# A mixture-of-experts stage in units of 32 slots instead of 64

## The chip, the cores and the metric

The kernel runs on one core of a Trainium2 chip. The metric is the device time of one execution in microseconds; the time before is 2393.91 us, the median of three runs (2392.5 to 2396.63). The profile shows one further execution. Engines are named PE (TensorE), DVE (VectorE), ACT (ScalarE), POOL (GpSimd) and SP (SyncE, which issues the DMAs of the weights).

## The reference

A float32 model of four mixer layers is followed by a second block: an adaptive norm, a hybrid mixer, and a layer of 32 experts of which each of the 256 tokens uses four. The change touches only the experts:

```
logits = xt @ w_router + b_router                  # 256 tokens x 32 experts
top_v, top_e = lax.top_k(logits, 4)
gates = softmax(top_v)
for each expert e, for its tokens:
    h = xt @ w1[e] + b1[e]                         # 1024 -> 2048
    gate, up = split(h);  gate = min(gate, 7);  up = clip(up, -7, 7)
    h = gate * sigmoid(1.702 * gate) * (up + 1)    # the swiglu, 1024 wide
    y[token] += gates[token, e] * (h @ w2[e] + b2[e])   # 1024 -> 1024
out = rms_norm(x + gate2 * y, final_norm)
```

How many tokens an expert gets is known only when the kernel runs. Each expert's w1 has 8 MB and its w2 4 MB.

## The kernel before

Everything up to the router (until about 1297 us) is the same in both kernels and is left out here. The expert stage walks over the experts in order (`for e in range(32)`, L1929 to L1964). The place of a token in an expert is a slot. The first 64 slots of an expert are always computed; slots 64 to 95, 96 to 127 and 128 upwards stand in branches that test the count `n` of the expert (`tc.If(n > 64)`, nested `n > 96` and `n > 128`), in `up_others` and `down_others`.

One expert goes through these steps:

- Gather: one-hot matrices P (token by slot, one column per slot) are multiplied with the tokens (`g<-P,xc`) for two experts at a time; the result, modulated, is `xq`, 64 slots of each.
- `up_proj`: slots (64 columns of the array) against w1. The bias of `b1` is the first product (`hg<-b1p,sel`). The 2048 columns of w1 are four blocks; with 64 slots two blocks lie on the two column halves of the array at once, and the result `hg` covers two banks, [128, 2, 512].
- swiglu on DVE and ACT into `um` [128, 512], four transposes of `um` into `aT` (`act_T`, L1739).
- `down_proj` of the expert before (`py<-w,aT`, L1748): two column halves; its output is scaled by the slots' gates (`slot_gates`, tile `gsq`) and by gate2, and split into two parts `yeh` and `yel`.
- `scatter`, once per pair of experts (even iterations): the transposed one-hots `gTq` times `yeh` and `yel` (`py<-yeh,gTq`) sum 128 slots over all rows of the array into the tokens' `y`, which lies in `xl`; DVE adds.
- A branch repeats the same in units of 32 slots, each block of w1 on a quarter of the columns (`hg<-w,xs`), with its own gather before it and its own sum behind it (`down_more`).

Weights come through a ring of 18 tiles of 1 MB: eight of w1 (`wload`, L1405) and four of w2 (L1411, L1418 for the last expert) for each expert, in the order w1[0], w1[1], w2[0], w1[2], w2[1] and so on, all issued by SP. A tile may be overwritten when its readers are done. For w1 that includes the branch: SP waits for the place where all engines are past the branch "up" of the expert (L1899, called its join here), for w2 for that of "down" (L1885). Into the same queue, ahead of the last four tiles of w1 of expert 31, goes the small load of the final norm's weights, `fr` (L1916), which waits for its own buffer.

The order of instructions on each engine is fixed when the kernel is built, by a scheduler with hints (`tc.issue_after`, `announce`). On each engine what stands behind a waiting instruction waits too.

Of the kernel before, what the change touches and what calls it, by code (L numbers as in the profile page):

```python
# [51 lines left out]
def tile_model(ctx: ExitStack, tc: tile.TileContext, A, out):  # L52
# [1368 lines left out]
    def w2_tile(e, kk, hh):  # L1421

        if e < 31:
            return w2s[e][kk // 2][:, kk % 2, hh * 512:(hh + 1) * 512]
        return w2s[e][2 * hh + kk // 4][:, kk % 4, :]
# [31 lines left out]
    def gate_halves():  # L1457

        g2 = rt["g2"] = rt["pool"].tile([128, 512], F32, name="g2")
        p = rtile(1, 512)  # L1460
        for b in range(2):
            mm(p[64 * b:64 * b + 64], selg[:, 2 * b:2 * b + 1].to_broadcast([128, 64]), mods[5][2])
        evac(g2, p)
# [97 lines left out]
    def new_P():  # L1561
        return rt["pool"].tile([128, 2, 128], F32, name="P2", tag="P2")
# [3 lines left out]

    def block(hg, b):
        if len(hg.shape) == 2:  # L1570
            return hg[32 * b:32 * b + 32, :], 32
        return hg[64 * (b % 2):64 * (b % 2) + 64, b // 2, :], 64

    def bias(e, hg):
        for b in range(4):
            o, n = block(hg, b)
            r = 4 * (e % 8) + b
            i = mm(o, rt["late"][1][:, r:r + 1].to_broadcast([96, n]), rt["late"][0][:, e // 8], True, False)
        return i
# [34 lines left out]
    def route():  # L1614
# [5 lines left out]
        with tc.issue_after(rt["last"].ins):  # L1620
            gather_first(0, 4)
            gate_halves()
# [14 lines left out]
    def experts(pos, gate, num):  # L1637
        h = xc
        with ExitStack() as st:
# [5 lines left out]
            def add_b2():  # L1645

                g2f = ep.tile([128, 1024], F32, name="g2f", tag="yeh")
                tmps = ep.tile([128, 1024], F32, name="tmps", tag="yel")
                for b in range(2):
                    p = gtile()  # L1650
                    mm(p, ident[:, 64 * b:64 * b + 1].to_broadcast([128, 128]), g2)
                    evac(g2f[:, b * 512:(b + 1) * 512], p)
                g4, gT = [tmps[:, 512 * i:512 * i + 512].rearrange("p (a b) -> p a b", b=128) for i in range(2)]
                V.memset(g4, 0.0)
                for t in range(2):
                    tp = gtile()
                    for c in range(4):
                        V.tensor_copy(g4[:, c, 32 * c:32 * c + 32], gate[:, t])
# [34 lines left out]
            def transposed(P, dst):  # L1693

                p = gtile()
                for t in range(2):
                    T.transpose(p[:, t * 128:(t + 1) * 128], P[:, t], ident)
                evac(dst, p[:, 0:256])

            def slot_gates(P, e, gs):  # L1700

                p = gtile()
                for j in range(2):
                    for t in range(2):
                        for hh in range(2):
                            mm(p[64 * hh:64 * hh + 64, j:1 + j], P[:, t, slices(j)], gate[:, t, e + j:e + j + 1], t == 0, t == 1)
                V.tensor_copy(gs, p[:, 0:2])
# [11 lines left out]
            def up_proj(w1, hg, xs, k0=0, k1=8):  # L1719
                for k in range(k0, k1):  # L1720
                    for b in range(4):
                        i = mm(block(hg, b)[0], xs[:, k, :], w1[k][:, b * 512:(b + 1) * 512], False, k == 7)
# [20 lines left out]
            def down_proj(aT, e, gs, take):  # L1743

                p = ytile()
                for kk in range(8):
                    for hh in range(2):
                        i = T.matmul(p[64 * hh:64 * hh + 64, :], aT[:, kk % 4, 64 * (kk // 4):64 * (kk // 4) + 64],  # L1748
                                     w2_tile(e, kk, hh), start=kk == 0, stop=kk == 7)
                        if kk == hh == 0:  # L1750
                            announce(i, f"down{e}")
                for hh in range(2):
                    sl = slice(hh * 512, (hh + 1) * 512)
                    rs = slice(64 * hh, 64 * hh + 64)
                    take(sl, p[rs, :], gs[rs], g2[rs])
                return i

            def scatter(gT, ye):

                for t in range(2):  # L1760
                    for hh in range(2):
                        sl = slice(hh * 512, (hh + 1) * 512)
# [26 lines left out]
            def act_more(hgs, g, um):  # L1789
                swiglu(hgs[g][0:64], hgs[g][64:128], um[half(g)], half(g))  # L1790

            def down_more(e, j, g, um, ps):
# [5 lines left out]
                p = ps[1]  # L1798
                for kk in range(8):
                    for hh in range(2):  # L1800
                        r = 64 * hh + 32 * (kk % 2)
                        i = mm(p[r:r + 32, :], aT1[:, kk % 4, 32 * (kk // 4):32 * (kk // 4) + 32],
                               w2_tile(e, kk, hh), kk < 2, kk > 5)
                        if kk == hh == 0:
                            first = i
                P1 = new_P1()
                for t in range(2):
                    at = ep.tile([128, 1], F32, name="ats", tag="ats")
                    V.tensor_scalar(at, pos[:, t, e:e + 1], -float(64 * j + 32 * g), None, ALU.add)
                    for i in range(2):  # L1810
# [415 lines left out]
```

## Time and profile before

| | before |
|---|---|
| time, median of 3 runs | 2393.91 us |
| profiled execution | 2408.4 us |
| its span | 2406.5 us |
| granted TensorE clock, mean | 0.96 |
| TensorE busy | 2226.5 us, 93% |
| VectorE busy | 1188.2 us, 49% |
| ScalarE busy | 725.9 us, 30% |
| up projection, `hg<-w,xq` | 500.2 us in 2048 instructions |
| down projection, `py<-w,aT` | 221.3 us in 992 instructions |

The matmuls of float32 stand twice in the trace for each one in the program, so 64 rows of the trace are 32 products. A matmul's time in a timeline is from its start to a modelled end, and several run at once in different parts of the array. Shares over the whole span say little here, as the stages differ; what counts is the expert stage from 1297 us on.

### The profile page before, as it was taken

To read this page: it belongs to the slowest core of one execution; us is meant where nothing else is said; L and a number is where in the kernel's file an instruction comes from. 1 tells how busy PE (TensorE), PEld (TensorE's weight loads), DVE (VectorE), ACT (ScalarE), POOL (GpSimd) and SP (SyncE) were. 2 spreads that over 40 slices of the span, in tenths; PEclk is the share of its full clock that TensorE was granted. 3 is DMA by queue.
4 is the path that set the end of the run, shared out by engine and by line. 5 is a ranking of instruction groups with operands and counts; after the bars stand their busy time and mean duration, and the time that the engine had idled before them with its cause. 6 is when DMAs were issued, how large, how long until landed. Compare 5 with 4: busy or idle time off the path is not lost. (4 is left out here: it accounts for less than half of the span.)

```text
span 2406.5 us, 32540 instructions
## 1 busy us (share of the span) xinstructions
PE 2226.5 (93%) x12516; PEld 1372.9 (57%) x12516; DVE 1188.2 (49%) x2545; ACT 725.9 (30%) x1588; POOL 79.8 (3%) x125
## 2 busy tenths in 40 slices
PE   7999999999999999998998899989989899999997
PEld 4767777777788887677864343333334333334342
DVE  3877666656666669867544123232323333322332
ACT  3555454345333456554232011010111110101101
POOL 0000010000000010002200000000000000000000
PEclk9999999999999999999999899999989989999998
DMA  8443432333333245646237978787999868999995
GB/s 305 132 149 127 136 119 78 98 125 125 115 102 122 80 127 180 206 162 249 80 111 305 371 312 351 281 350 278 413 414 415 333 257 354 378 413 413 413 377 230
DMA packets 124828, 576.71 MB, mean 240 GB/s; under 512 B 11953, under 2 KB 12721, under 8 KB 91762
## 3 DMA queue, kind: packets, MB, share of 16 engines
q1 hardware_dynamic: 124530, 572.71, 62.5%
q8 instruction: 190, 3.11, 0.5%
q14 instruction: 108, 0.88, 0.1%
HBM read 571.61 MB, written 1.05 MB: 238 GB/s over the span
## 5 line engine op out<-in xcount | busy, mean ns | idle before, releaser
L136 PE MATMUL hg<-w,xq 128*64 128x512 f32 x2048 | 500.2, 621 | 15.2 <-PEq L1899 6.7
L136 PE MATMUL mm<-hT,wp 128*128 128x256 f32 (+1 forms) x1776 | 351.2, 342 | 0.6 <-DVE aqk L144 0.5
L136 PEld LDWEIGHTS hg<-w,xq 128*64 128x64 f32 x2048 | 161.1, 143 | 323.3 <-issue 306.3
L136 PEld LDWEIGHTS mm<-hT,wp 128*128 128x128 f32 x1776 | 272.5, 190 | 54.2 <-issue 19.8
L1729 DVE TENSOR_SCALAR gm<-hg 128x512 f32<-128x512 f32 (+1 forms) x37 | 25.6, 691 | 436.2 <-PE hg L136 434.6
L1748 PE MATMUL py<-w,aT 128*64 128x512 f32 x992 | 221.3, 592 | 1.1 <-DMA w<-w 1.0
L111 DVE TENSOR_TENSOR wp<-w,wp 128x1024 fp32r<-128x1024 f32 (+2 forms) x149 | 178.7, 1204 | 75.5 <-ACT wp L110 72.1
L136 PE MATMUL mm<-wp,hT 128*128 128x256 f32 (+1 forms) x1584 | 198.1, 284 | 5.1 <-DVE mixT L419 3.0
L136 PEld LDWEIGHTS mm<-wp,hT 128*128 128x128 f32 x1584 | 191.0, 191 | 11.0 <-DVE mixT L419 3.2
L110 ACT ACTIVATE wp<-w 128x1024 fp32r<-128x1024 f32 (+2 forms) x149 | 153.8, 1035 | 101.3 <-PE mm L136 55.2
L1730 ACT ACTIVATE um<-gm 128x512 f32<-128x512 f32 x32 | 20.2, 630 | 528.8 <-DVE gm L1729 528.8
L1748 PEld LDWEIGHTS py<-w,aT 128*64 128x64 f32 x992 | 84.3, 137 | 131.0 <-issue 118.9
L110 ACT ACTIVATE yeh<-gm 64x512 fp32r<-64x512 f32 x62 | 39.0, 628 | 202.3 <-DVE gm L1872 202.1
L1872 DVE SCALAR_TENSOR_TENSOR gm<-py,gsq,g 64x512 f32<-64x512 f32 x62 | 46.5, 750 | 100.1 <-PE py L1748 99.1
L136 PE MATMUL ada<-w,scT 128*32 128x512 f32 x576 | 83.6, 625 | 5.8 <-DMA w<-l_w_ada 5.7
L136 PEld LDWEIGHTS g<-P,xc 128*128 128x128 f32 x496 | 57.8, 191 | 24.8 <-issue 24.8
L136 PE MATMUL g<-P,xc 128*128 128x128 f32 x496 | 63.8, 281 | 1.1 <-DVE P L1678 1.1
L136 PE MATMUL hg<-w,xs 128*32 128x512 f32 x480 | 60.0, 650 | 5.0 <-DVE xs L144 3.8
L136 PE MATMUL s<-wp,oz 128*128 128x512 f32 x264 | 64.1, 392 | 0.0
L1766 DVE TENSOR_TENSOR xl<-xl,py 128x512 f32<-128x512 f32 x60 | 39.7, 686 | 41.8 <-PE py L136 38.2
L136 PEld LDWEIGHTS s<-wp,oz 128*128 128x128 f32 x264 | 49.1, 188 | 13.3 <-issue 2.5
L587 ACT ACTIVATE e<-e,nm 128x512 f32<-128x512 f32 x64 | 45.7, 716 | 30.9 <-DVE nm L586 30.7
(606 smaller groups left out, 3039.6 us busy)
## 6 DMA issues: line engine op xcount, KB each, us to landing
w<-w SPq DMA_DIRECT2D x383, 1024.0 KB, 15.5
w<-l_w_ada SPq DMA_DIRECT2D x96, 512.0 KB, 4.3
w<-w_ada SPq DMA_DIRECT2D x48, 512.0 KB, 4.4
w<-l_w_z SPq DMA_DIRECT2D x32, 512.0 KB, 4.6
w<-l_w_out SPq DMA_DIRECT2D x32, 512.0 KB, 4.2
w<-l_w_q SPq DMA_DIRECT2D x16, 512.0 KB, 5.3
w<-l_w_v SPq DMA_DIRECT2D x12, 512.0 KB, 5.0
w<-w_dqkv SPq DMA_DIRECT2D x12, 512.0 KB, 4.4
```

The source lines that it names most:

```text
L110: S.activation(hi, src, AF.Copy)
L111: V.tensor_tensor(lo, src, hi, op=ALU.subtract)
L136: return T.matmul(o, l, r, start=start, stop=stop)
L587: S.activation(e, e, AF.Exp, scale=0.125, bias=nm[:, c:c + 1], accum_out=den[:, c:c + 1])
L1729: V.tensor_scalar(gm, gate, 7.0, None, ALU.min)
L1730: S.activation(um, gm, AF.Sigmoid, scale=1.702)
L1748: i = T.matmul(p[64 * hh:64 * hh + 64, :], aT[:, kk % 4, 64 * (kk // 4):64 * (kk // 4) + 64], w2_tile(e, kk, hh), start=kk == 0, stop=kk == 7)
L1766: V.tensor_tensor(y[:, t, sl], y[:, t, sl], py, op=ALU.add)
L1872: V.scalar_tensor_tensor(w, p, gs, g2, ALU.mult, ALU.mult)
```

## The change

The unit becomes 32 slots. The first 32 slots of an expert are computed always, each of four column blocks on a quarter of the array's columns, so `hg` needs one bank instead of two. Slots 32 to 63 move into the branch, behind `n > 32`, ahead of those over 64, 96 and 128: in "up" they read w1 once more from the ring, and their swiglu goes to the second half of `um`; in "down" they have their own product, their own transposed one-hots (`four`) and their own sum (`sum_more`). The down projection has four quarters of 256 columns. The scatter sums 32 rows at a time, on row quarters, in four banks. Gates and transposes of P are made by quarters too. `fr` and two temporaries of `add_b2` move to buffers of the branches (`ums1`), and `fr` stands two tiles earlier in SP's queue.

The core of the diff:

```
-    def new_hg(e):
-        hg = rt["pe"].tile([128, 2, 512], F32, name="hg", tag="hg")
+    def htile():
+        return rt["pe"].tile([128, 512], F32, name="hg", tag="hg", bufs=2)
...
+            def four(o, P, t, s0, r, start=True, stop=True):
+                for c in range(4):
+                    mm(o[quarter(c)], P[:, t, s0:s0 + 32], r, start, stop)
...
-            def down_proj(aT, e, gs, take):
-                p = ytile()
+            def down_proj(p, aT, e, c0=0, cs=range(4)):
+                first = None
                 for kk in range(8):
-                    for hh in range(2):
-                        i = T.matmul(p[64 * hh:64 * hh + 64, :], aT[:, kk % 4, 64 * (kk // 4):64 * (kk // 4) + 64],
-                                     w2_tile(e, kk, hh), start=kk == 0, stop=kk == 7)
+                    for c in cs:
+                        i = mm(p[quarter(c)], aT[:, kk % 4, c0 + 32 * (kk // 4):c0 + 32 * (kk // 4) + 32], w2_tile(e, kk, c), kk == 0, kk == 7)
+                        first = first or i
+                return first, i
...
+            def scatter(gTs, yes):
+                ps = [ytile() for _ in range(2)] + [gtile() for _ in range(2)]
                 for t in range(2):
-                    for hh in range(2):
-                        py = ytile()
-                        for i, part in enumerate(ye):
-                            mm(py, gT[:, t * 128:(t + 1) * 128], part[:, sl], i == 0, i == len(ye) - 1)
-                        V.tensor_tensor(y[:, t, sl], y[:, t, sl], py, op=ALU.add)
+                    for j in range(2):
+                        for i, part in enumerate(yes):
+                            for c in range(4):
+                                mm(ps[c][:, 256 * t:256 * t + 256], gTs[quarter(c), j, 128 * t:128 * t + 128], part[quarter(c), j], i + j == 0, i + j == 2)
+                for c in range(4):
+                    take_in(c, ps[c])
...
+            def sum_more(P, s0, p, gs, bks):
+                tp = bks[0]
+                for t in range(2):
+                    four(tp[:, t * 128:(t + 1) * 128], P, t, s0, ident)
+                evac(gT1, tp[:, 0:256])
...
+                for c in range(4):
+                    to = bks[c % len(bks)]
+                    for t in range(2):
+                        mm(to[:, 256 * t:256 * t + 256], gT1[quarter(c), 128 * t:128 * t + 128], ye1[quarter(c)])
+                    take_in(c, to)
...
-                with tc.If(n > 64, label=f"down{e}"):
-                    if hg is not None:
-                        mm(hg[:, 0, 0:1], ident, ident[:, 0:1])
-                    announce(down_more(e, 1, 0, ums[:, 0], ps), f"down{e}.1")
+                with tc.If(n > 32, label=f"down{e}"):
+                    p = ps[1][:, 0:256]
+                    announce(down_proj(p, aT, e, 64)[0], f"down{e}.1")
+                    bks = ps if hg is None else [ps[0], hg, ps[1]]
+                    j = e % 2
+                    sum_more(Pq[e // 2], 64 * j + 32, p, gTs[e // 2][1][:, 2 * j + 1:2 * j + 2], bks)
+                    with tc.If(n > 64, label=f"down{e}.1"):
...
-                with tc.If(n > 64, label=f"up{e}"):
-                    announce(gather_more(e, 1, ps[1]), f"up{e}.1")
-                    up_more(e, ps, 0)
-                    act_more(ps, 0, ums[:, 0])
+                with tc.If(n > 32, label=f"up{e}"):
+                    announce(bias(e, ps[0]), f"up{e}.1")
+                    up_proj(w1s[e], ps[0], xq[e // 2][:, :, 64 * (e % 2) + 32:64 * (e % 2) + 64])
+                    act_more(ps, 0, um, 1)
+                    with tc.If(n > 64, label=f"up{e}.1"):
...
-                up_proj(w1s[e], hg, xq[e // 2][:, :, slices(e % 2)])
+                i = up_proj(w1s[e], hg, xq[e // 2][:, :, 64 * (e % 2):64 * (e % 2) + 32])
...
-                swiglu(hg[:, 0], hg[:, 1], um)
+                act_more([hg], 0, um)
...
-                    last = down(e - 1, aT)
-                    with tc.issue_after(last.ins):
-                        aT = between()
-                    down_others(e - 1, nxt)
+                    down(e - 1, aT)
+                    down_others(e - 1, aT, nxt)
...
+                aT = act_T(um)
+                if e < 30:
+                    prep(e // 2 + 1, e % 2)
```

How the instructions move, at three places. First PE, between the branch "up" of expert 11 and the branch "down" of expert 10. Here `g<-cb,um` are the transposes of the activation, `g<-P,xc` the gather, `g<-gate,P` the gates and `g<-cb,P` the transposes of the one-hots. Before:

```order
L136 MATMUL hg<-w,xq 64x512 x4
L1748 MATMUL py<-w,aT 64x512
L2222 BRANCH_PREFETCH_HINT
L1748 MATMUL py<-w,aT 64x512 x15
L136 MATMUL g<-P_20527,xc 128x128 x8
L136 MATMUL g<-gate,P_20527 64x1 x8
L1697 MATMUL g<-cb,P_20527 128x128 x2
L1739 MATMUL g<-cb,um 128x128 x3
L1885 COMPARE_AND_BRANCH
```

and after the change, on the same engine at the same place:

```order
L136 MATMUL hg<-w,xq 32x512 x4
L136 MATMUL py<-w,aT 32x256 x8
L1748 MATMUL g<-cb,um 128x128 x4
L136 MATMUL g<-P_23632,xc 128x128 x6
L136 MATMUL py<-w,aT 32x256 x8
L136 MATMUL g<-P_23632,xc 128x128 x2
L136 MATMUL py<-w,aT 32x256 x8
L136 MATMUL g<-gate,P_23632 32x1 x32
L136 MATMUL g<-cb,P_23632 32x128 x16
L136 MATMUL py<-w,aT 32x256 x8
L1878 COMPARE_AND_BRANCH
```

The transposes of the activation moved from the end of this stretch to behind the first 8 of 32 products of the down projection, and gates and one-hot transposes became 48 instructions where there were 10.

Second, what PE does after the change at the head of the taken branch "down" of an expert (`hg_24190`, `hg_24191` and `hg` are three banks, `xs` here holds the transposed one-hots):

```order
L1878 COMPARE_AND_BRANCH
L136 MATMUL hg_24191<-w,aT 32x256
L2217 BRANCH_PREFETCH_HINT
L136 MATMUL hg_24191<-w,aT 32x256 x31
L136 MATMUL hg_24190<-cb,P_21526 32x128 x8
L136 MATMUL hg_24190<-ye_24235,xs_12630 128x256 x2
L136 MATMUL hg<-ye_24235,xs_12630 128x256 x2
L136 MATMUL hg_24191<-ye_24235,xs_12630 128x256 x2
L136 MATMUL hg_24190<-ye_24235,xs_12630 128x256 x2
L1884 COMPARE_AND_BRANCH
```

The second half of the expert's slots has a down projection of its own here, which before was part of the 64 columns outside the branch; the branch for more than 64 slots begins behind it.

Third, SP near the end of the weights, before:

```order
L1405 DMA w<-w_2 128x2048
L1916 DMA fr<-fnorm 1x1024
L1405 DMA w<-w_2 128x2048 x4
L1411 DMA w<-w_2 128x2x1024
```

and after:

```order
L1917 DMA ums_12629<-fnorm 1x1024
L1405 DMA w<-w_2 128x2048 x6
L1411 DMA w<-w_2 128x2x1024
```

The small load stands ahead of six of the last eight w1 tiles instead of four, and its buffer is one of the branches' instead of the one of `yeh`.

## Rows read from the trace of the kernel before

**Rows 1.** Windows: stretch, its length, busy per engine, clock, DMA share, GB/s

```profile
1740.00:1800.00 60.00, 53.69 (x250) 22.94 (x248) 16.73 (x30) 6.69 (x12) 0.00 (x0) 0.89 1.02 414
1920.00:1980.00 60.00, 53.76 (x311) 22.01 (x311) 21.80 (x48) 7.46 (x15) 0.00 (x0) 0.90 0.64 257
```

**Rows 2.** Timeline of SP's queue, w1 tiles: start, duration, line, operation, count

```profile
1340.83 27.57 SPq L1405 DMA_DIRECT2D w<-w  x8
...
1715.99 23.07 SPq L1405 DMA_DIRECT2D w<-w  x8
...
1842.27 30.52 SPq L1405 DMA_DIRECT2D w<-w  x8
...
2103.46 25.26 SPq L1405 DMA_DIRECT2D w<-w  x8
...
2321.76 7.75 SPq L1405 DMA_DIRECT2D w<-w  x4
...
2354.23 2.08 SPq L1405 DMA_DIRECT2D w<-w  x4
```

**Rows 3.** Timeline of PE, an odd iteration: start, duration, operation, idle before

```profile
1710.72 1.94 PE L136 MATMUL hg<-w,xq 128*64 128x512 f32 x8
1712.46 7.07 PE L1748 MATMUL py<-w,aT 128*64 128x512 f32 x32
1719.46 2.05 PE L136 MATMUL g<-P,xc 128*128 128x128 f32 x16
1721.44 0.63 PE L136 MATMUL g<-gate,P 128*64 128x1 f32 x16
1723.43 0.44 PE L1697 MATMUL g<-cb,P 128*128 128x128 f32 x2 [1.36 <-DVE gsq L1707]
...
1738.28 1.94 PE L136 MATMUL hg<-w,xq 128*64 128x512 f32 x8 [0.16 <-PEq L1899]
...
1769.05 1.94 PE L136 MATMUL hg<-w,xq 128*64 128x512 f32 x8
```

**Rows 4.** What SP waited for: total us, times, longest

```profile
SPq L1405 <- PEq L1899: 219.4, 21, 19.0
```

**Rows 5.** Timeline of PE, the taken branch "up" of expert 4

```profile
1435.95 0.39 PE L136 MATMUL hg<-b1p,sel 96*32 96x512 bf16 x1
...
1440.56 7.07 PE L136 MATMUL hg<-w,xs 128*32 128x512 f32 x64 [0.18 <-DVE xs L1509]
1448.11 1.94 PE L136 MATMUL hg<-w,xq 128*64 128x512 f32 x8 [0.48 <-PEq L1903]
```

**Rows 6.** Timeline of DVE, two swiglus in series

```profile
1447.70 0.68 DVE L1729 TENSOR_SCALAR gm<-hg 64x512 f32<-64x512 f32 x1 [4.74 <-PE hg L136]
...
1450.58 0.68 DVE L1733 SCALAR_TENSOR_TENSOR ums<-ums,gm 64x512 f32<-64x512 f32 x1
1451.67 0.69 DVE L1729 TENSOR_SCALAR gm<-hg 128x512 f32<-128x512 f32 x1 [0.41 <-DVEq L1903]
```

**Rows 7.** Timeline of PE, branches "down" of experts 4 and 7

```profile
1493.92 5.22 PE L136 MATMUL hg<-w,xs 128*32 128x512 f32 x32 [0.77 <-DVE xs L144]
...
1617.63 3.72 PE L136 MATMUL hg<-w,xs 128*32 128x512 f32 x32 [0.97 <-DVE xs L144]
1621.28 0.66 PE L136 MATMUL hg<-cb,P 128*64 128x128 f32 x8
1622.82 1.13 PE L136 MATMUL hg<-ye,xs 64*128 64x512 f32 x4 [0.88 <-DVE ye L1818]
1624.69 1.72 PE L136 MATMUL hg<-ye,xs 64*128 64x512 f32 x4 [0.74 <-DVE xl L1824]
```

**Rows 8.** Timeline of PE, the scatter of an even iteration

```profile
1751.32 0.50 PE L136 MATMUL py<-yeh,gTq 128*128 128x512 f32 x1 [1.35 <-ACT yeh L110]
```

**Rows 9.** Windows: a stretch in which PE often waits

```profile
1320.00:1330.00 10.00, 4.46 (x14) 1.58 (x14) 0.79 (x2) 1.40 (x3) 0.00 (x0) 0.66 1.02 415
```

**Rows 10.** Timeline of PE, behind a branch not taken

```profile
1892.08 1.06 PE L136 MATMUL hg<-b1p,sel 96*64 96x512 bf16 x4 [6.21 <-PEq L1885]
```

More of the change, by code (lines that the diff above doesn't have):

```diff
@@ L1455, in rtile, with quarter, gate_quarters @@
         return rt["pe"].tile([128, 512], F32, name=f"hg{g}", tag=f"hg{g}")[:, 0:n]
[L1457 to L1462, printed above, removed]
+    def quarter(c):
+        return slice(32 * c, 32 * c + 32)
+    def gate_quarters():
+        g2 = rt["g2"] = rt["pool"].tile([128, 256], F32, name="g2")
+        p = rtile(1, 256)
+        for c in range(4):
+            mm(p[quarter(c)], selg[:, 2 * (c // 2):2 * (c // 2) + 1].to_broadcast([128, 32]), mods[5][2][:, 256 * (c % 2):256 * (c % 2) + 256])
         evac(g2, p)
@@ L1797, in down_more @@
                 evac(aT1.rearrange("p a b -> p (a b)"), tp[:, 0:256])
[L1798 to L1805, printed above, removed]
+                p = ps[1][:, 0:256]
+                first, _ = down_proj(p, aT1, e)
                 P1 = new_P1()
@@ L1840, in prepare_sum @@
             def prepare_sum(q):
[L1841 removed]
+                gs = ep.tile([128, 4], F32, name="gsq", tag="gsq", bufs=2)
                 slot_gates(Pq[q], 2 * q, gs)
[L1843 to L1857 removed]
+                gT = ep.tile([128, 2, 256], F32R, name="gTq", tag="gTq", bufs=2)
@@ new lines, in take, with finish @@
+            def take(hh):
+                return V.scalar_tensor_tensor(yl[half(hh)], p[half(hh)], gs[half(hh), 2:3], g2[half(hh)], ALU.mult, ALU.mult)
+            def finish(c):
+                for t in range(2):
+                    mm(sums[c][:, 256 * t:256 * t + 256], gT[quarter(c), t * 128:(t + 1) * 128], yl[quarter(c)], False, t == 1)
+                return take_in(c, sums[c]).ins
+            yl = ep.tile([128, 256], F32, name="yl")
+            down_proj(p, aT, 31, 0, (0, 1))
+            sums = [htile() for _ in range(2)] + [gtile() for _ in range(2)]
@@ new lines, in experts @@
+            ye = yes.pop(15)
+            for t in range(2):
+                for i, part in enumerate(ye):
+                    for c in range(4):
+                        mm(sums[c][:, 256 * t:256 * t + 256], g30[quarter(c), 0, t * 128:(t + 1) * 128], part[quarter(c), 0], i + t == 0, False)
+            take(0)
+            i, last = down_proj(p, aT, 31, 0, (2, 3))
+            announce(i, "down31")
+            with tc.issue_after(i.ins):
+                finish(0)
+            with tc.issue_after(last.ins):
+                finish(1)
@@ L2018, in experts @@
+            down_others(31, aT)
+            i = take(1)
             with tc.issue_after(i.ins):
@@ L2021, in experts @@
                 times_fn(0)
-            with tc.issue_after(finish(1, range(2))):
+            finish(2)
+            i = finish(3)
+            for t in range(2):
+                squares(t, 1)
+            with tc.issue_after(i):
                 times_fn(1)
```

227 lines of the change are left out of this document (87 added, 140 removed).

## The prediction

> **What bounds the kernel now.** Only the expert stage changes, so I read from there on: first the windows, for the share of each engine and of the DMA; then SyncE's timeline, which shows the pace of the weights; then its waits; last TensorE's and VectorE's timelines, instruction by instruction.
>
> Between 1740 and 1800 us TensorE is busy 53.69 us of 60 and the DMA is full at 414 GB/s; between 1920 and 1980 TensorE is as busy and the weights come at only 257 GB/s [rows 1]. So two limits lie close together, and which one holds changes from expert to expert. Feeding: from 1715.99 to 1842.27 SyncE starts the w1 tiles of four experts, 126.28 us, or 31.57 us each with a DMA that never stops [rows 2]. Computing: one join of a branch "up" to the next takes 27.56 us in an odd iteration and 30.77 us in an even one, mean 29.2 [rows 3]. An expert of up to 64 slots is thus computed a little faster than it is fed, and one of more slots is not. The ring of 18 tiles absorbs the difference until it is full of tiles that can't be released; then SyncE stands still, as in its 21 waits of 219.4 us in all for the join at L1899 [rows 4], and DMA time is lost that nothing gives back.
>
> That lost time can be summed from the starts of w1 [rows 2]. From 1340.83 to 1715.99 lie ten experts: 375.2 us against 315.7 us of feeding, 59.5 lost. From 1842.27 to 2103.46 lie seven: 261.2 against 221.0, 40.2 lost. From 2103.46 to 2321.76 lie seven more: 218.3 against 221.0, nothing lost. The reference's router on its own inputs says why; the slots of experts 0 to 31 are 43, 5, 62, 35, 67, 7, 5, 100, 15, 9, 38, 12, 17, 42, 18, 41, 95, 54, 71, 33, 60, 20, 29, 28, 6, 19, 14, 3, 21, 46, 3, 6. The two stretches that lose contain the four experts over 64 (4 and 7; 16 and 18). Over 32 there are 14: five of the first eight, all of 15 to 20, and 10, 13 and 29.
>
> **The change part by part.** A light expert (32 slots or fewer) becomes cheaper, one of 33 to 64 dearer, because its second half is a whole unit in a branch.
>
> Light iteration after the change. The 32-wide up projection has its price in the branch of before: 7.07 us [rows 5]. The transposes of the activation now stand after only a quarter of the down projection (shown for TensorE in the order of the change), so TensorE waits there for the swiglu: from the start of its first operation to the end of its last it takes 3.56 us on 64 partitions (1447.70 to 1451.26) [rows 6], and counting 0.2 for its start, 0.85 of the 3.5 us of down projection lies beside it; 2.9 remain. The Trainium skill, "TensorEngine Tiling (Array Packing)", section PSUM Bottleneck, says that tiling speeds up TensorE but not the emptying of its banks. By that rule the swiglu stays at 3.56 however few the slots are, and the trace agrees: 0.68 against 0.69 us for one operation on 64 and on 128 partitions [rows 6]. Were it halved with the slots, an iteration would be some 1.8 us shorter and the rule would be no obstacle. The sum: up 7.07, wait 2.9, transposes 0.6, down 3.5 (3.72 is the row of the 32-wide one [rows 7]; four column quarters of half the width, same columns in all), gather 2.05 [rows 3], bias 0.4 [rows 5]: 16.5. An odd iteration adds the gates, 64 instructions by 0.63/16 or 2.1 to 2.5, the transposes of P, 0.9 (bound 2.6 by the 0.66 for eight [rows 7]), and the 1.36 wait for gsq [rows 3]: 20.9. An even one adds the scatter: 1.35 of waiting [rows 8] and 32 products of a quarter's rows and 256 columns, between 2 us (four at a time) and 8 us (one by one at half of 0.50); I take 4, as the row quarters share the array but write four banks: 21.9. Mean 21.3, bounds 18 (waits hidden by work that the hardware overlaps) and 24.
>
> Second half, 33 to 64 slots. In branch "up": bias 0.39, up 7.07, join 0.48 [rows 5] and 0.3 to enter: 8.3. Its swiglu and that of the first half then run in series on VectorE, 3.56 more, of which 0.75 lies beside work: 2.8. In branch "down": product 3.5 (3.72 and 5.22 are the rows), one-hot transposes 0.4 to 0.66, evacuation and scaling 0.9, eight sum products with VectorE's additions between them 3.2 (1.13, 0.74 and 1.72 make 3.6 in the branch of before [rows 7]), join 0.45: 8.3, bounds 6.5 and 9.5. Together 19.4, so such an expert takes 40.7 where it took 29.2. The units over 64 keep their matmuls: 22.5 for the third (in before 12.2 in up, 1435.95 to 1448.11 [rows 5], and about as much in down), 17.9 for the fourth. So 63.2 for 65 to 96 slots and 81.1 for expert 7.
>
> The walk. Carry from expert to expert how far the join lags behind the weights: add the expert's time, subtract 31.5; the lag can't fall below 3 (TensorE then waits for the weights), and above about 23 the ring is full (ten tiles by 31.57/12 = 2.63, less some 3 to restart): what is over is lost. Starting at 5, experts 0 to 3 bring 14.2, 4.0, 13.2, 22.4. Expert 4 loses 31.1. Experts 5 and 6 bring the lag down to 3, and expert 7 loses 29.6: together 61, where 59.5 were lost before. Experts 8 to 14 sit near 3 to 12; their gain, ten us each, has nothing to go to, as the feeding sets the pace. Expert 15 goes to 12.2, 16 loses 20.9, 17 loses 9.2, 18 loses 31.7, 19 and 20 lose 9.2 each, and the 5 us of add_b2 at expert 20 are lost too: 85, where 40.2 were. After expert 20 nothing is lost in either kernel. The same walk on before, with its own times, gives some 61 where the rows show 100, since the lag of before recovers more slowly than it says; after the change the light experts recover ten us each, so that there the entry into the second stretch is little in doubt, and the loss within it is TensorE's own sum.
>
> Around it. At the start the place of the nineteenth tile is freed at the join of up(0), and expert 0 has 43 slots, so its branch is taken: between 0 and 9 later, I take 6. At the end the load of fr keeps SyncE from the last four w1 tiles: from 2321.76 to 2356.31 instead of 23 us [rows 2], some 11.5 lost. Now it waits for buffers long free, but still behind the join of the branch down: between nothing and those 11.5 gained, I take 5. Tail after the last weight: unchanged within 2.
>
> Sum: (61 + 85) - 100 + 6 - 5 = +47. On the profiled execution's 2408.4 us that is 2455; the median of the runs shown, 2393.91, is 14.5 lower, so I forecast a time of 2441. What a measurement can tell from no change is 0.2%, or 4.8 us.
>
> **Rivals.** A, the feeding hides it all (faster): the light iteration costs 18 and the surcharge 14, nearly the bare matmuls (7.07 and 3.5 twice). The walk then loses 53 + 5: 58 - 100 + 1 = -41, 2353. For it: light experts gain ten us each against the feeding, and the ring absorbs 20. Against: the swiglu wait stands in TensorE's own order, and every bound has to fall low at once. It decides at a light time of 19.9 with a surcharge of 16 (92 + 5 lost): below that the kernel is faster. B, about equal: near that point, 2389 to 2399. C, worse: the granted clock falls in the new waits. It was 0.66 where TensorE was busy 4.46 us of 10 [rows 9], and 32 products of a down branch took 5.22 us at one place and 3.72 at another [rows 7]. If the 10.6 us of matmuls of the second half take 40% longer in the nine taken experts that run at a full ring (4, 7, 16 to 20 and the two ahead of them), that is 4.2 by 9, +38: 2479. Beside it, a late fetch of instructions after a branch (6.21 us in one place, [rows 10]) now has 14 taken branches of each kind to happen in.
>
> **How the numbers follow.** The forecast's own case, 2415 to 2470, has 0.60; C and worse, above 2470, 0.18; between 2399 and 2415, 0.07; B 0.05; A 0.10. Faster 0.10, same 0.05, slower 0.85. The range leaves out a tenth on either side: 2396 (the walk at 19.9 and 16) to 2490 (C, with two late fetches).
>
> **What would show it.** Right: in the profile after, SyncE's starts of w1 keep 31.5 us in experts 8 to 14 and 21 to 30, and stretch to some 40 for experts 17, 19 and 20; TensorE is idle some ten us per light expert, released by the DMA of w; a join to join of 40 for a taken expert at a full ring; the transposes of um preceded by an idle time of about 3 us released by VectorE. Wrong: if the DMA stays near 414 GB/s from 1850 to 2050, the surcharge is under 15 and A holds; if taken experts need more than 45 us, C; if light experts without a full ring take above 25, my sum of small pieces was short.

## The result and the profile after

The changed kernel takes 2674.52 us (median of four runs, 2661.44 to 2680.88) where the kernel before takes 2394.34: the ratio is 1.1163, with a 95% interval of 1.1118 to 1.1207. The direction was forecast, the size was not: 47 us were expected and 280 came, far outside the range of 2396 to 2490.

| | before | after |
|---|---|---|
| time of the profiled execution | 2408.4 us | 2680.88 us |
| its span | 2406.5 us | 2679.1 us |
| granted TensorE clock, mean | 0.96 | 0.898 |
| TensorE busy in the whole span | 2226.5 us | 2268.7 us |
| TensorE busy from 1300 us on | 995.5 us | 1037.8 us |
| ... of it lost at half clock (worked out below) | 47 us | 210 us |
| TensorE idle from 1300 us on | 110 us | 341 us |

The third line from the bottom comes from one row of the windows of each kernel. First before, then after: stretch, length, busy time of PE, PEld, DVE, ACT and POOL, clock, DMA share, GB/s.

```profile
1300.00:2406.00 1106.00, 995.55 (x5002) 408.94 (x5001) 329.86 (x625) 118.97 (x224) 1.99 (x4) 0.94 0.88 352
```

```profile
1300.00:2679.00 1379.00, 1037.76 (x10022) 531.13 (x10014) 349.51 (x670) 105.79 (x209) 1.99 (x4) 0.82 0.70 281
```

The granted clock has two levels, 1.2 and 2.4 GHz, which stand as 0.5 and 1.0. I went through the same stretches in windows of 1 us and summed busy time by one minus the clock: what TensorE would have saved at the full level. That sum is 47 us before and 210 after. So TensorE's work, counted at full clock, fell by 120 us (948.5 to 828), as the light experts should bring; it pays 163 us more at half clock and is idle 231 us more.

SyncE's queue shows where the feeding was lost; these rows answer to [rows 2].

```profile
1327.50 38.18 SPq L1405 DMA_DIRECT2D w<-w  x8
...
1808.26 33.60 SPq L1405 DMA_DIRECT2D w<-w  x8
...
1878.78 28.54 SPq L1405 DMA_DIRECT2D w<-w  x8
...
2357.57 19.07 SPq L1405 DMA_DIRECT2D w<-w  x8
...
2576.65 2.69 SPq L1405 DMA_DIRECT2D w<-w  x2
...
2622.93 0.29 SPq L1917 DMA_DIRECT2D ums<-fnorm  x1
2623.29 3.21 SPq L1405 DMA_DIRECT2D w<-w  x6
```

Ten experts from 1327.50 to 1808.26 took 480.8 us against 315.7 of feeding: 165 lost (before 59.5). The next two took 70.5, 7 lost. The nine from 1878.78 to 2357.57 took 478.8 against 284.1: 195 lost (before 40.2). The last seven lose nothing. Together 367 where the prediction had 146 and the rows of before 100: nearly the whole of the 272 by which the profiled executions differ.

What a taken expert does in that time is seen best in one iteration. This is PE's timeline after the change, from the join of expert 16's branch "up" to that of expert 17 (54 slots); it answers to [rows 3, 5, 7].

```profile
2013.36 1.07 PE L136 MATMUL hg<-w,xq 128*32 128x512 f32 x8 [0.57 <-PEq L1904]
2014.24 1.05 PE L136 MATMUL py<-w,aT 128*32 128x256 f32 x16
...
2020.40 1.12 PE L1748 MATMUL g<-cb,um 128*128 128x128 f32 x4 [4.68 <-DVE um L1742]
2021.45 4.55 PE L136 MATMUL py<-w,aT 128*32 128x256 f32 x48
...
2027.38 3.66 PE L136 MATMUL hg<-w,aT 128*32 128x256 f32 x64
2030.86 0.62 PE L136 MATMUL hg<-cb,P 128*32 128x128 f32 x16
2032.02 1.16 PE L136 MATMUL hg<-ye,xs 32*128 32x256 f32 x12 [0.55 <-DVE xs L144]
2033.93 1.13 PE L136 MATMUL hg<-ye,xs 32*128 32x256 f32 x4 [0.75 <-DVE xl L1764]
2035.49 0.62 PE L136 MATMUL hg<-b1p,sel 96*32 96x512 bf16 x4 [0.44 <-PEq L1884]
...
2036.77 3.78 PE L136 MATMUL g<-P,xc 128*128 128x128 f32 x16
...
2053.86 7.04 PE L136 MATMUL hg<-w,xq 128*32 128x512 f32 x62
2061.57 1.06 PE L136 MATMUL hg<-w,xq 128*32 128x512 f32 x8 [0.67 <-PEq L1900]
2062.45 1.05 PE L136 MATMUL py<-w,aT 128*32 128x256 f32 x16
```

The reader sees two matmul groups that cost 7.04 and 3.66 us, as the prediction had priced them (7.07 and 3.5), and between them the same kind of work at 1.7 to 1.8 times its cost: the gather of 16 takes 3.78 us where [rows 3] has 2.05, and 48 of the down projection take 4.55 where 64 in the branch take 3.66. The windows of the same iteration show the clock at these places.

```profile
2016.00:2019.00 3.00, 0.00 (x0) 0.00 (x0) 1.86 (x4) 0.63 (x1) 0.00 (x0) 0.87 1.03 429
2019.00:2025.00 6.00, 4.60 (x40) 2.44 (x44) 1.31 (x2) 0.00 (x0) 0.00 (x0) 0.50 1.01 409
2026.00:2035.00 9.00, 7.09 (x100) 4.35 (x100) 3.58 (x7) 1.01 (x2) 0.00 (x0) 1.00 0.99 403
2036.00:2048.00 12.00, 12.00 (x56) 8.12 (x56) 4.13 (x10) 0.91 (x2) 0.00 (x0) 0.50 0.88 352
2049.00:2061.00 12.00, 11.90 (x114) 3.37 (x106) 0.04 (x1) 0.00 (x0) 0.00 (x0) 1.00 0.01 1
```

TensorE waits 4.68 us for the swiglu, the clock falls to 0.50, and 4.60 us of busy time behind the wait run at half level. The short waits of the branch "down" follow, the clock falls once more, and 12 us of work run at half level; that these waits are the cause is my reading, as no run takes them away. Join to join the iteration takes 48.2 us; half of 4.60 and of 12.00 is 8.3; without the clock it would be 39.9, and 40.7 was forecast. In the last window the DMA stands still (1 GB/s): the ring is full, and each of these microseconds is lost.

A further item is in the waits of PE after the change (us in all, times, longest).

```profile
PE g L1748 <- DVE um L1742: 101.6, 31, 5.2
PE hg L136 <- issue: 48.2, 14, 6.6
PE hg L136 <- PEq L1878: 33.2, 14, 4.6
...
PE hg L136 <- PEq L1896: 14.8, 14, 4.2
```

The first is the wait for the swiglu. Its mean of 3.3 us mixes two kinds: 13 waits of 4.4 to 5.2 us, where the expert has a second half and two swiglus run in series (2.9 and 2.8 were forecast, 5.7 together), and 18 of up to 2.9 us, 2.1 on average (2.9 forecast). So the waits were no longer than forecast. The second, time in which the profile shows nothing that PE waits for, is 4.0 us in three in the kernel before. In expert 3's branch "down" it stands behind 11 of the products:

```profile
1498.31 1.05 PE L136 MATMUL hg<-w,aT 128*32 128x256 f32 x11
1504.28 5.63 PE L136 MATMUL hg<-w,aT 128*32 128x256 f32 x51 [4.92 <-issue]
```

### The profile page after: what moved, and what is told of

It reads as the page before. It is cut to its first block, busy times and chain, and to the rows that moved or that the text cites. A ratio compares the mean times of both kernels' runs of the same rounds, so it can differ in the third digit from the quotient of the medians.

```text
span 2679.1 us, 43271 instructions
## 1 busy us (share of the span) xinstructions
PE 2268.7 (85%) x17714; PEld 1491.4 (56%) x17714; DVE 1208.1 (45%) x2598; ACT 714.7 (27%) x1578; POOL 80.8 (3%) x125
## 5 line engine op out<-in xcount | busy, mean ns | idle before, releaser
L136 PE MATMUL hg<-w,xq 128*32 128x512 f32 x2944 | 406.6, 664 | 40.6 <-PEq L1896 14.8
L136 PEld LDWEIGHTS hg<-w,xq 128*32 128x32 f32 x2944 | 112.5, 120 | 281.6 <-issue 236.5
L1738 DVE TENSOR_SCALAR gm<-hg 64x512 f32<-64x512 f32 x51 | 34.8, 683 | 416.3 <-PE hg L136 410.7
L111 DVE TENSOR_TENSOR wp<-w,wp 128x1024 fp32r<-128x1024 f32 (+2 forms) x149 | 177.7, 1198 | 71.7 <-ACT wp L110 70.5
L136 PE MATMUL py<-w,aT 128*32 128x256 f32 x2048 | 163.0, 445 | 6.5 <-issue 3.5
L136 PEld LDWEIGHTS py<-w,aT 128*32 128x32 f32 x2048 | 73.3, 128 | 85.4 <-issue 54.9
L136 PE MATMUL g<-P,xc 128*128 128x128 f32 x496 | 102.5, 381 | 20.7 <-issue 12.9
L1748 PE MATMUL g<-cb,um 128*128 128x128 f32 x128 | 30.4, 382 | 101.6 <-DVE um L1742 101.6
L136 PEld LDWEIGHTS g<-P,xc 128*128 128x128 f32 x496 | 94.0, 287 | 31.3 <-issue 26.7
L136 PE MATMUL hg<-w,aT 128*32 128x256 f32 x896 | 64.5, 429 | 32.1 <-issue 32.1
L136 PE MATMUL hg<-w,xs 128*32 128x512 f32 (+1 forms) x640 | 72.8, 615 | 3.1 <-ACTq L1886 1.1
L136 PE MATMUL hg<-ye,xs 32*128 32x256 f32 x304 | 53.0, 442 | 26.2 <-DVE xl L1764 14.3
```

The costliest lines, as they stand in the source:

```text
L111: V.tensor_tensor(lo, src, hi, op=ALU.subtract)
L136: return T.matmul(o, l, r, start=start, stop=stop)
L1738: V.tensor_scalar(gm, gate, 7.0, None, ALU.min)
L1748: T.transpose(tp[:, q * 128:(q + 1) * 128], um[:, q * 128:(q + 1) * 128], ident)
```

## The experiments

The theory formed from these rows: the forecast's own work is about right, but (clock) each wait for the swiglu, and each cluster of short waits, takes the granted clock down for the work behind it, and (late instructions) the hints, which announce to PE that a branch skips its body, are wrong at 14 experts now instead of four, so that bodies start late. The rival: the second halves themselves cost far more than 19.4 us, and clock and waits lie beside the feeding. The table has the time of each kernel, and from its trace, from 1300 us on, the waits for um, PE's idle time without a releaser ("issue") inside `hg` groups and in all groups, and the loss at half clock, worked out as above.

| kernel | time us | waits for um | `hg` <- issue | all <- issue | lost at half clock |
|---|---|---|---|---|---|
| before | 2394 to 2397 | none | 4.0 | 7.1 | 47 |
| after | 2674.52 | 101.6 | 48.2 | 69.8 | 210 |
| late | 2538.11 | 27.7 | 31.5 | 63.5 | 149 |
| spare | 2626.69 | 13.3 | 50.6 | 65.7 | 150 |
| hints | 2629.36 | 102.9 | 5.5 | 29.5 | 192 |
| later | 2505.04 | 1.8 | 1.5 | 27.4 | 165 |
| best | 2508.12 | 27.4 | 5.3 | 49.2 | 162 |
| skip | 2464.23 | 71.4 | 13.5 | 48.5 | 168 |
| no128 | 2649.48 | 100.2 | 57.5 | 63.7 | 189 |
| b_wait | 2498.69 | 65.8 | 6.1 | 8.7 | 69 |
| b_wait4 | 2605.51 | 118.2 | 0.3 | 0.6 | 134 |

**late: the transposes behind the down projection.** `act_tp` makes the four transposes.

```
...
-                    down(e - 1, aT)
+                    last = down(e - 1, aT)
+                    with tc.issue_after(last.ins):
+                        tp = act_tp(um)
...
-                aT = act_T(um)
+                aT = act_T(um, tp)
...
```

> The changed kernel, with the transposes of the activation behind all 32 products of the down projection instead of behind the first 8; nothing else. Clock theory (a wait of some 5 us for the swiglu takes the granted clock to half for the next 7 us or so of work, and that is most of what the forecast missed): the waits of TensorE for um, 101.6 us in 31, fall below 50, TensorE's work at half clock falls with them, and the time falls by 60 to 130 us, to 2545 to 2615. Surcharge theory (the second halves cost so much by themselves, the clock lies beside the feeding): only the wait's own length counts, and only in the some 16 iterations at a full ring: 2.6 us by 16, about 40, to 2635. Fetch theory (instructions come late in the taken branches): the same 40 or less.

Measured: 2538.11 us, ratio to before 1.0594 (1.0546 to 1.0643); 136 us less than after. The waits for um fell by 74 us and the loss at half clock by 61, together 135. The time lies 7 us below the clock theory's range (2545 to 2615), so that theory's sign is right and its size was too modest; the rival's 40 us is out. Wait and clock fell together here; the next run takes them apart.

**spare: work that nothing reads, in the wait.**

```
...
+                    if kk == 1 and spare is not None:
+                        with tc.issue_after(i.ins), tc.high_priority():
+                            for _ in range(SPARE):
+                                mm(spare[:, 0:256], ident, g2)
...
```

`SPARE` is 7.

> The changed kernel, with seven products of 128x256 that nothing reads in the wait for the swiglu (their bank is started anew afterwards): the wait stays as long, but TensorE works in it. Clock theory: work behind the wait runs at full clock again, 3.3 us less in each of some 16 iterations at a full ring, and 40 to 80 us less in all, though TensorE does 3.5 us more per expert. Surcharge and fetch theory: nothing gained, the products can only delay: 0 to 30 us more.

Measured: 2626.69 us, 48 less than after, though TensorE is busy 44 us more. The swiglu itself was not touched; only what TensorE does beside it changed. The same place in an iteration now (expert 17): PE's timeline, where the fourteen rows of `hg<-g,cb` are the added work,

```profile
2046.14 3.29 PE L136 MATMUL hg<-g,cb 128*128 128x256 f32 x14
2049.36 1.07 PE L136 MATMUL py<-w,aT 128*32 128x256 f32 x16
2051.36 0.63 PE L1748 MATMUL g<-cb,um 128*128 128x128 f32 x4 [0.93 <-DVE um L1742]
...
2058.67 5.01 PE L136 MATMUL hg<-w,aT 128*32 128x256 f32 x64
```

and the windows over it and behind it:

```profile
2046.00:2052.00 6.00, 5.07 (x40) 3.66 (x37) 4.01 (x6) 0.63 (x1) 0.00 (x0) 1.00 1.00 407
2052.00:2058.00 6.00, 4.79 (x116) 3.22 (x119) 1.53 (x5) 1.33 (x3) 0.00 (x0) 1.00 1.02 414
```

The transposes take 0.63 us instead of 1.12, the clock stays at 1.00 over the 6 us behind them, and useless work makes the kernel 1.8% faster. This separates the clock from the wait. The gain is not whole: in the last row the product of the branch "down", which stands behind three shorter waits (0.93, 0.93 and 0.28 us), takes 5.01 us, where the iteration shown of the changed kernel had 3.66. In all the loss at half clock falls by 60 of the 163 us that the change had added.

**hints: none where the body runs.** With `OVER` the 14 experts over 32 slots:

```
             def announce(after, label):
+                if int(label.lstrip("updown").split(".")[0]) in OVER and "." not in label:
+                    return
                 with tc.issue_after(after.ins):
```

> The changed kernel without the two prefetch hints (that the branch skips its body) at the 14 experts whose bodies run; the other 18 keep theirs. Fetch theory: TensorE's idle time inside those bodies that nothing in the profile releases, 48.2 us in 14, goes, and with it the half clock behind it: 50 to 100 us less. Clock theory with the swiglu waits alone as its cause: within 15 us of the changed kernel. Surcharge theory: the same.

Measured: 2629.36 us, 45 less, which lies between the two expectations (50 to 100 less, and within 15). The idle time without a releaser went from 48.2 to 5.5 us inside `hg` groups and from 69.8 to 29.5 in all, the loss at half clock from 210 to 192. Expert 3's body "down" now starts without the standstill shown above; all 64 in one piece:

```profile
1485.84 3.66 PE L136 MATMUL hg<-w,aT 128*32 128x256 f32 x64
```

So the hints made the standstill; that it is the body's code that came late is a reading which no row shows. The waits behind the outer joins stayed (34.0 us in 16 where 33.2 in 14 stood, and 21.8 in 14 where 14.8 in 14 stood), so they have another cause.

**b_wait: the same early transposes in the kernel before.** The four transposes stand behind two of eight steps of the down projection; the unit is still 64 slots.

```
...
+                for kk in range(2):
+                    i = step(kk)
+                with tc.issue_after(i.ins):
+                    tps[0], i = act_tp(um)
+                with tc.issue_after(i.ins):
+                    for kk in range(2, 8):
+                        i = step(kk)
...
```

> The kernel before, with the transposes of the activation moved up behind the first quarter of the down projection, as they stand after the change; its unit stays 64 slots. Clock theory: each iteration gets a wait of 2.7 us for the swiglu and 3 us of half clock behind it, so an expert of up to 64 slots takes 35 us, above the feeding: 32 by 4 to 6 less what the ring absorbs, 80 to 160 us more, and the mean clock falls from 0.96 to below 0.92. Surcharge theory: only the wait, some 2.7 us less the 2 per expert by which the feeding is slower: 20 to 50 us more, at an unchanged clock.

Measured: 2498.69 us, 103 more than before (1.0412, 1.0363 to 1.0461), but with a mean clock of 0.957: the time fits the clock theory's range and the clock doesn't. The waits are 65.8 us and the loss at half clock rose by only 21, so most of the time lost here is the waits' own length; the scheduler also moved part of the up projection behind the branch "up". Around two waits of the same length:

```profile
1785.14 1.92 PE L1755 MATMUL py<-w,aT 128*64 128x512 f32 x8
1788.96 0.66 PE L1738 MATMUL g<-cb,um 128*128 128x128 f32 x4 [1.91 <-DVE um L1733]
1789.55 5.37 PE L1755 MATMUL py<-w,aT 128*64 128x512 f32 x24
...
1851.45 0.66 PE L1738 MATMUL g<-cb,um 128*128 128x128 f32 x4 [1.91 <-DVE um L1733]
1852.04 7.07 PE L1755 MATMUL py<-w,aT 128*64 128x512 f32 x24
```

```profile
1789.00:1795.00 6.00, 6.00 (x29) 2.17 (x30) 0.03 (x1) 0.03 (x1) 0.00 (x0) 1.00 1.01 413
```

The windows row is for the first: behind 1.91 us of waiting the clock is 1.00. Behind the second the same 24 rows take 7.07 us instead of 5.37. Of the 27 waits of 1.90 to 2.00 us in this trace, 13 have a clock of 1.00 over the 6 us that follow and 14 have 0.72. So the theory as I had put it, that any such wait brings the clock down, was too wide; but a wait of this length doesn't leave it alone either, as the next expectation says. What separates the 13 from the 14 stays open. The next run asked for the longer wait.

**b_wait4: the transposes ahead of the whole down projection**, the edit of b_wait without its first loop.

> The kernel before with the transposes of the activation ahead of the whole down projection: the same edit as b_wait, with the quarter of the down projection that covered some 1.9 us of the swiglu taken away, so that each wait is near 4 us instead of 2.0. Length alone (a wait costs its microseconds): 31 by 1.9, 50 to 60 us above b_wait, 2550 to 2560, at the same share of half clock. Clock theory (a wait of 2 us leaves the granted clock alone, one of 4 to 5 us takes it down): TensorE's time lost at half clock rises from 69 us in b_wait to 110 or more, the mean clock falls below 0.94, and the time comes to 2580 to 2630.

Measured: 2605.51 us, 107 more than b_wait, with a mean clock of 0.93. Waits grew by 52 us and the loss at half clock by 65. The answer in rows:

```profile
1823.50 0.66 PE L1738 MATMUL g<-cb,um 128*128 128x128 f32 x4 [3.62 <-DVE um L1733]
1824.09 8.78 PE L1755 MATMUL py<-w,aT 128*64 128x512 f32 x32
```

```profile
1820.00:1823.00 3.00, 0.00 (x0) 0.00 (x0) 2.24 (x4) 0.63 (x1) 0.00 (x0) 1.00 0.97 404
1823.00:1829.00 6.00, 5.50 (x20) 2.02 (x22) 0.45 (x1) 0.00 (x0) 0.00 (x0) 0.72 1.02 420
```

The down projection takes 8.78 us where [rows 3] has 7.07, and the clock over it is 0.72. Of the 28 waits of 3.6 to 3.7 us, 25 have a lower clock over the 6 us that follow (0.50 to 0.75) and three have 1.00: the longer wait brings the clock down more often, not always. The Trainium skill, "TensorE: Matmul & The Clock Gate", section HAM oscillation, describes a kernel whose array falls back to the lower level in every round of a loop that waits for DMA between its bursts. The trace of the changed kernel agrees for the waits of its taken experts, though they are for VectorE: over the 6 us behind each of the 13 waits of 4.4 to 5.2 us the clock was between 0.52 and 0.76.

**skip: no second halves at ten experts.** The outer test of both branches is `n > 64`, so slots 32 to 63 of these ten are left out.

> The changed kernel with the outer test of both branches at more than 64 slots instead of more than 32: slots 32 to 63 of the ten experts with 33 to 64 are left out, and those experts run like light ones; the four over 64 run as in the changed kernel. It prices the second halves of the ten. By the prediction's walk (19.4 us each, absorbed in part) the lost feeding falls from 146 to 75: 70 us less than the changed kernel, some 2600. If a taken expert costs what the trace of the changed kernel shows (45 to 50 us join to join at a full ring, clock and late instructions included), all that the ten cost above the feeding goes, ten by 14 to 18, with two of them absorbed: 130 to 180 less, 2495 to 2545. Light experts near 21 us of TensorE time would bring it as low as the kernel before; above 2450 they are not enough to win even without second halves.

Measured: 2464.23 us, 210 less than after, ratio to before 1.0272 (1.0241 to 1.0303). Ten second halves cost 21 us each in the time of the kernel; the forecast's walk would have given 70. That is more than either expectation. It is not the second halves alone: at these ten experts the hints are now right, and the idle time without a releaser in `hg` groups fell with them, from 48.2 to 13.5 us. And with them gone the kernel still doesn't beat the one before: the loss at half clock is still 168 us, the waits for um 71.4.

**later: no wait for the swiglu at all.** The transposes stand behind the branch "down", and the hints are as in hints.

```
...
-                    announce(bias(e + 1, nxt), f"up{e + 1}")
-                aT = act_T(um)
+                    i = bias(e + 1, nxt)
+                    announce(i, f"up{e + 1}")
+                with tc.issue_after(i.ins):
+                    aT = act_T(um)
...
```

> The changed kernel with the transposes of the activation behind the branch down instead of ahead of it, and without the prefetch hints at the 14 experts whose bodies run. No wait for the swiglu is left: the branch of the expert before, or the products behind it, cover it. If the account so far holds (waits for um 28 us and some 15 us of half clock still in the run late, 45 for the hints), 2538 less 28, 15 and 45: 2450, or up to 2490 if they overlap. If the unit of 32 slots were only held up by its waits, it would come under 2400.

Measured: 2505.04 us, ratio to before 1.0465 (1.0424 to 1.0506), above the expected 2450 to 2490. The waits for um are 1.8 us, those without a releaser in `hg` 1.5, yet 165 us are lost at half clock. What is left of waits are the short ones in the branches, those behind the outer joins (45.9 us in 15 at L1882, 21.6 at L1900) and 23.7 us without a releaser that now stand in groups of `g`, where the changed kernel had 13.3. That these bring the clock down by themselves is likely and not shown.

**best: three edits at once** (late, hints, and the load of `fr` issued by ScalarE).

> The changed kernel with three things at once: the transposes of the activation behind the whole down projection, no prefetch hints at the 14 experts whose bodies run, and the load of the final norm's weights in ScalarE's queue instead of SyncE's. If the three causes (wait and clock, late instructions, the queue at the end) are separate they add: 136 and 45 from the runs so far and some 22 for the queue, 2470. If they share the same microseconds, 2500 to 2530. Under 2400 would say that the unit of 32 slots itself wins once the waits are gone; the surcharge theory says that it stays above 2440.

Measured: 2508.12 us (1.0467, 1.0426 to 1.0508), 38 above the sum: the causes share microseconds. It is the case "2500 to 2530". Part of it is in the table: without hints and with the transposes late, the idle time without a releaser left the `hg` groups (5.3 us) and came back in others (43.9 us in `g` and `py` groups, 21.6 in the changed kernel).

**no128: the bodies for over 128 slots left out.** The cut is from the branch "up"; "down" loses its body in the same way.

```
...
-                            with tc.If(n > 128, label=f"up{e}.3"):
-                                for j in (2, 3):
...
```

> The changed kernel without the bodies for more than 128 slots, none of which runs with these inputs; what is left out is code alone. Late instructions by distance (a jump over a long body lands in code that isn't loaded): the idle time of TensorE behind the joins L1878 and L1896, 33.2 and 14.8 us in 14 each, falls by half or more, 20 to 45 us less. If the number of branches or the wrong hints are the cause, and not the length: within 10 us of the changed kernel.

Measured: 2649.48 us (2640.3 to 2664.53), some 25 less than after (2661.44 to 2680.88, in another set of runs). That lies between its two expectations (20 to 45 less, and within 10). But the waits behind the outer joins did not halve: 37.5 in 17 and 15.7 in 13, against 33.2 and 14.8. The length of these bodies is not what makes them. Of the 25 us, the loss at half clock is 21 lower; why stays open.

**b_fr and b_hints: two edits on the kernel before.** The load of `fr` by ScalarE, and no hints at experts 4, 7, 16 and 18.

```
-                nc.sync.dma_start(fr, A["fnorm"])
+                nc.scalar.dma_start(fr, A["fnorm"])
```

> The kernel before with the load of the final norm's weights in ScalarE's queue instead of ahead of the last four w1 tiles in SyncE's. If SyncE's standstill there (2329.5 to 2353.9 in the trace before) holds the last weights up, they land some 11 us earlier and the time falls by 8 to 13 us, to 2381 to 2386. If the ring holds those tiles back anyway, no change. The kernel after should gain more by the same edit, as its load waits for the branch of expert 29.

> The kernel before without the prefetch hints at the four experts whose bodies run (4, 7, 16, 18). The wrong hints cost the changed kernel about 45 us at 14 experts, 3 each; four of them would give the kernel before 5 to 13 us, 2382 to 2390. If its wrong hints are free, as 4.0 us of idle time without a releaser in its trace suggest, no change.

Measured: 2397.89 us (ratio 0.9994, 0.9967 to 1.0021) and 2398.08 us (1.0011, 0.9991 to 1.0031). No change, either of them; the standstill of SyncE at the end of [rows 2] was not worth what I had put it at. No kernel here beats the one before.

## Why the prediction was wrong

What bounds the kernel was read rightly: the ring, two stretches of taken experts, the feeding of 31.5 us that takes back what light experts gain. The lost feeding grew in those stretches: 260 of the 267 us, the other 7 in the two experts between them.

The surcharge was right as work. "An expert takes 40.7 where it took 29.2": the one iteration shown has 39.9 at full clock, and 48.2 as it ran. At 65 to 96 slots 63.2 was forecast, and expert 18 took 82.3 (2062.45 to 2144.75 in PE's timeline), with 3.02, 2.88 and 1.95 us of late instructions and late data in it.

The step that failed is what the sum put at nothing: the clock behind the waits, and the late starts at the branches. Both were left outside the 40.7 and the 21.3, the first as rival C, "the granted clock falls in the new waits", wrong as a price and as a chance. I priced it as 40% more on "the 10.6 us of matmuls of the second half" in nine experts, 38 us. The rows show the clock down in whatever stands behind a wait: the down projection, the gather, the scatter and the next up projection, in light experts too. In the one iteration it is 8.3 us instead of 4.2; over the stage 163 us more than before. I had the row for it ([rows 9], 0.66 where PE is half busy) and applied it to the wrong instructions. spare shows that the clock is a cause and not only a companion, as with the wait left and filled the time falls; b_wait4 agrees, as with the wait lengthened the time rises by wait and clock together. What the two of spare and late show for the swiglu's waits is some 60 of the 163 us; that the rest lies behind the other waits is read from rows like those above and not tested.

The walk let light experts "bring the lag down" by ten us each, with 21.3 us for an iteration; that failed too. Behind the second stretch lie six iterations of light experts in a row, from one group of transposes to another:

```profile
2357.80 0.66 PE L1748 MATMUL g<-cb,um 128*128 128x128 f32 x4 [2.33 <-DVE um L1742]
...
2460.85 0.40 PE L136 MATMUL hg<-b1p,sel 96*32 96x512 bf16 x4 [3.41 <-PEq L1878]
...
2536.55 0.67 PE L1748 MATMUL g<-cb,um 128*128 128x128 f32 x4 [1.91 <-DVE um L1742]
```

They take 178.75 us, 29.8 each, between 23.0 and 33.6, and TensorE waits for w in one place of them (3.9 us). The sign that I had named for the sum of a light expert being short, "above 25", came; the sign for it being right, "idle some ten us per light expert, released by the DMA of w", did not: such waits are 12.3 us in 8 places in the whole stage. In these six, 26.5 us were lost at half clock and 22.5 spent in waits behind the outer joins (the row in the middle is one): 4.4 and 3.8 us each. Without them and the wait for w an iteration has 20.9, where 21.3 was forecast. So the light expert was right as work as well, and both its extras were put at nothing.

The prediction's own walk says how much each is worth (an estimate from these rows): 146 us lost as forecast; 281 with the taken experts as they ran (48.2; 82.3 over 64 slots, and 17.9 more over 96); 195 with light ones at 29.1 alone; 339 with both. Measured were 360 in the two stretches. The two add up to more than each alone because a light expert that gains two us on the feeding instead of ten leaves the lag to the next taken one, and at a full ring each microsecond counts.

Late instructions stood in the prediction as "Beside it", at two times 6.21 us. The 48.2 us in 14 places had their cause in the code for all to see: a hint that the body is skipped, at 14 experts that run it. Taking the hints away gave 45 us.

Of the small terms, the start was put at 6 later; w1 of expert 3 starts at 1327.50 instead of 1340.83, but 11 us of that exist before the expert stage begins (the five tiles at 1277.25 start at 1266.30), so it is 2 earlier. The end was put at 5 gained, and SyncE's last w1 tiles came at 2626.5, 49.9 us after the first of them instead of 34.5: the load waited 43.1 us for the join of expert 29's branch "down", which has 46 slots and is taken. The buffer was free, as I said; what I had called "still behind the join" was the whole of it. And b_fr shows that the 11.5 us that I had put on this load in the kernel before were not there to be gained.

Two rivals fell: A (the feeding hides it) and B (about equal) needed light experts at 18 to 20 us. Two slips in the prediction's working change nothing: the items of its branch "down" add up to 8.45 us or more where 8.3 is written, and the 5.22 and 3.72 us of rival C belong to 32 rows, which are 16 products.

What stays open: what makes TensorE wait behind the outer joins (33.2 and 14.8 us) when neither the hints nor the bodies for over 128 slots move it; why one wait of two us brings the clock down and another doesn't; and how much of the last 110 us between later and before would go if the short waits of the sums were filled as well, which wasn't tried.

## What to carry to other kernels

A wait of TensorE costs its length and can cost, behind it, the work that then runs at half clock, and the longer waits did so more often; when work is cut into smaller units, list every wait that used to lie under the larger unit's matmuls, in the light and in the heavy case, and charge the matmuls behind it too. When a branch goes from rarely to often taken, change its hints with it. And a saving in the experts that the feeding limits is worth only what the ring keeps of it for the next heavy one, while a microsecond more in those that fill the ring counts in full: weigh them by the actual sizes, one by one.

## What the runs showed of the hardware

- Fourteen rows of matmuls whose result nobody reads, put into a wait, made a kernel 48 us faster (2674.52 to 2626.69), at a clock of 1.00 over the 6 us behind them in the iteration shown, where the changed kernel's had 0.50.
- Two kernels that differ in the place of four transposes had waits of 1.9 to 2.0 and of 3.6 to 3.7 us. Behind 14 of 27 of the short ones the clock was down over the next 6 us (0.72), behind 25 of 28 of the long ones (0.50 to 0.75). The account by wait and half clock gives 118 us for the difference of the two kernels, and 107 were measured.
- Behind four waits of 0.44 to 0.75 us in a row the clock was 0.50 for 12 us (one iteration of the changed kernel; no run takes these waits away).
- Without the wrong hints at 14 experts, two each, the kernel was 45 us faster, some 1.6 us a hint (an estimate, 45 by 28); at four experts of the kernel before nothing could be measured.
- In light experts TensorE waited 3.8 us an iteration behind branches whose body is skipped (22.5 us in six), which neither hints nor shorter bodies took away.
